# A hybrid decoder layer: another half-product pair, fewer working tiles per attention head, and earlier sums at the output

## The chip, the cores and the metric

The kernel runs on one core of one Trainium2 chip. The metric is the device time of one execution in microseconds (us); smaller is better. The times of before are 1003.48, 1003.79 and 1007.32 us, so the median is 1003.79 us. The profile is of one further execution that took 1006.68 us, with a span of 1005.0 us.

## The reference

One decoder layer on 528 tokens (16 meta tokens and 512 others) of 2048 values. The normed input goes through one input projection; its columns feed three kinds of heads side by side; each head's output is multiplied by its own SiLU gate; all are joined and go through one output projection, and a last norm follows.

```python
h = rms_norm(x, norm_w)
proj = h @ w_in
(dq, dk, dv, dz, db, da, gq, gk, gv, gz, gl, fq, fk, fv, fz, ff) = split_cols(proj)
o_dn  = gated_head_norm(gated_delta_rule_chunked(...), dz, dn_norm_w)     # 6 heads of 128
o_gla = gated_head_norm(gla_chunked(...), gz, gla_norm_w)                 # 5 heads, keys 64, values 128
log_f = log_sigmoid(ff + b_f)
o_fox = forgetting_attention(fq * FOX_D**-0.5, fk, fv, log_f) * silu(fz)  # 5 heads of 128
return x + concatenate([o_dn, o_gla, o_fox]) @ w_out                      # then rms_norm(., final_norm_w)
```

`forgetting_attention` is softmax(q.k + c_t - c_s) over earlier positions, c the running sum of log f, in blocks of 128 queries.

## The kernel before

**Arithmetic.** Everything is float32, made of exact parts: a weight half-block (`raw`, 128 x 1024) becomes a rounded part on ScalarE (`whi`, L165) and the remainder on VectorE (`wlo`, L166), and each product is three matmuls: `xh whi`, `xl whi`, `xh wlo`. The input transposed lies in 16 tiles `xh`, `xl`, one for each 128 of the 2048 values, 528 columns wide; `HT` = 264 is half of them, `NM` = 16 the meta tokens. `load_half` (L144) issues the load of a half-block on the SP queue and the split; the pool `wp` has two buffers, so a third load waits until the first has been split. An ordinary block of 128 columns of `w_in` (`inproj`, L274) takes two half-blocks.

**Pairs by seven products.** For two column blocks of one attention head, `inproj_pair` (L578) does not multiply each by itself. It treats the upper and lower half of the 2048 values, the two token halves and the two blocks as a 2 x 2 by 2 x 2 matrix product, and does it with seven half-size products (`product`, L586, 24 matmuls of 264 columns) instead of eight. The operands are sums: of weights, in `ti` in DRAM, made long ahead by copies and accumulating transfers on the POOL queue; of inputs, in `t1`, `t2`, `t4` (`x_sums`, L541), and, last, `x_last` (L562). The latter overwrites the upper token half of the first eight `xh`, `xl` with a sum, so it comes after every block that still reads the plain input. Per 128 values it issues a load `xe` on the POOL queue, a scaling on ScalarE, a sum on VectorE, a cast on ScalarE into `xh` and a remainder on VectorE into `xl`. The results of the products land in banks of `psb` (four) named `pp_a`, `pp_b` and so on, and are added up into the head's tiles with two half-width intermediates `ta`, `tb` of the tile `tmp`.

**Stages.** Gates, DeltaNet and GLA come first, with their blocks; then the attention ("fox") heads 0 to 4. `fox_head(0)` projects head 0's four blocks in the ordinary way and, in between, the keys and queries (`fk`, `fq`) of head 1. `SKIP = 1` says that this is so: the list `PAIRS` of seven pairs begins with head 1's values and gate (`fv`, `fz`), then (`fk`, `fq`) and (`fv`, `fz`) of heads 2, 3 and 4. While a pair multiplies, the attention of the head before it runs among its matmuls: scores `pfa`, `pfd`, softmax `fp`, transposes `pfx`, output `pfo`. The scores of GLA's third pair of heads (`pss20` to `pss26`, on VectorE the gate differences and weighted keys `gvt`, `gpr`, `kq`) run among head 1's keys and queries. Two working tiles come from the pool `six` (14 buffers) for a head's probabilities, and one more, `fc`, for its gate row `cb`, masked rows `cm` and gate `z`.

**The output.** The first three column blocks of 512 (`pa`, cc 0 to 2) multiply the heads that are done, in four banks of `psb`; then VectorE adds each bank to `accs`, which was loaded with the residual input (`begin`, L1393, `add`, L1416). The rest of the output projection uses seven products too (`pq`, `pr`, `ps`), with weight sums `tw` in DRAM. The norm ends it (L1555 on).

**What sets the order.** Each engine runs its instructions in one fixed order. A scheduler lays that out from the written order and from priorities; weight splits and what is `paced` by them have high priority. On TensorE the products stand as written (`order`), and `PLACE` (L197) says behind which matmul of which block a small matmul may come. The weight-sum transfers are `chores`: each `load_half` allows `rate` units of them (a copy is 1, an accumulation 1.6), and `AHEAD` sets when which are queued and the rate:

```python
AHEAD = {(0, -1): (1.4, (-1, -2, -3, -4, -5, -6, -7), (0, 1, 2, 3))}
tc.add_manual_dep(x.ins, kqs[-1].name, ..., reason="behind")   # x_last: VectorE's part behind GLA's last score
for tb in range(4):
    add(tb, cc, pa[tb])
```

## Time and profile before

| | before |
|---|---|
| median of three runs | 1003.79 us |
| the profiled execution, its span | 1006.68 us, 1005.0 us |
| granted TensorE clock | 0.994 of full |
| TensorE busy | 984.8 us (98%), 7774 matmuls |
| VectorE busy | 658.0 us (65%) |
| ScalarE busy | 478.9 us (48%) |
| GpSimd busy | 251.0 us (25%) |
| gates, DeltaNet, GLA, head 0's blocks | 0 to 612.5 us |
| head 1's keys and queries | 612.5 to 638.5 us |
| the seven pairs | 638.5 to 813.8 us |
| output projection and norm | 813.8 us to the end |

PE is TensorE, DVE VectorE, ACT ScalarE, POOL GpSimd, SP the queue that issues the weight loads. A row of a group gives busy time, mean ns of one, and the idle time before its instructions with what ended it. A row of a timeline gives start, duration, engine, line, operation, output and inputs, and in brackets the idle time before it. Matmuls overlap each other, so the step from start to start, not the duration, is what one costs.

### The profile page before, as it was taken

How to read it: one execution, taken by the hardware profiler on the slowest of the kernel's cores; microseconds unless marked ns; L12 is line 12 of the kernel's file. 1: busy time of each engine (PE TensorE's matmuls, PEld its weight loads, DVE VectorE, ACT ScalarE, POOL GpSimd, SP SyncE). 2: the span in 40 equal slices, each digit the busy share in tenths (PEclk: the TensorE clock that was granted, in tenths of full speed). 3: DMA queues.
4: the chain of work that ended last, by engine and by line, in shares of the span. 5: the costliest groups of instructions: out<-in, count | busy, mean ns of one | idle time of the engine just before them, and what ended most of it. 6: DMA issues, size and time to landing. Idle time of an engine off the chain costs nothing.

```text
span 1005.0 us, 19758 instructions
## 1 busy us (share of the span) xinstructions
PE 984.8 (98%) x7774; PEld 899.4 (89%) x7774; DVE 658.0 (65%) x1427; ACT 478.9 (48%) x1045; POOL 251.0 (25%) x288
## 2 busy tenths in 40 slices
PE   9999999999999999999999999999999998999996
PEld 7899999898999888899999988898999986878885
DVE  5456786966667895335665848666766674968573
ACT  6753534334455244244444445655555552554254
POOL 0031523322233344212223123121212153000060
PEclk9999999999999999999999999999999999999998
DMA  9754666776546798734848685654454558448434
GB/s 338 264 192 165 210 214 234 172 195 158 126 111 171 152 220 220 265 121 149 229 106 218 156 210 161 197 175 145 149 181 145 189 183 296 149 155 272 138 105 168
DMA packets 67489, 186.05 MB, mean 185 GB/s; under 512 B 13725, under 2 KB 16973, under 8 KB 66692
## 3 DMA queue, kind: packets, MB, share of 16 engines
q1 hardware_dynamic: 41920, 121.86, 35.3%
q0 software_dynamic: 16576, 56.83, 23.7%
q10 hardware_dynamic: 8900, 6.10, 2.2%
q8 instruction: 61, 1.00, 0.4%
q14 instruction: 32, 0.26, 0.1%
HBM read 174.07 MB, written 56.69 MB: 230 GB/s over the span
## 4 chain that ended last, share of the span: by engine, by line
PE 80%; DMA 3%; DVE 3%; ACT 2%; issue 1%; POOL 0%; ACTq 0%; POOLq 0%; DVEq 0%
PE pp L260 38%; PE pp_a L592 8%; PE pa L1403 5%; PE pq L1403 4%; PE pt L1403 4%; PE ps L1403 2%; PE pp_b L592 2%; PE pp_d L592 2%; PE pp_c L592 2%; PE pss L1061 1%; PE pr L1403 1%; DMA xb<-in_xT 1%; PE pfo L1283 1%; PE pfa L1249 1%; DVE wlo L166 1%
## 5 line engine op out<-in xcount | busy, mean ns | idle before, releaser
L260 PE MATMUL pp<-xh,wlo 128*128 128x264 f32 (+2 forms) x1120 | 272.3, 306 | 1.4 <-DVE wlo L166 1.4
L260 PE MATMUL pp<-xh,whi 128*128 128x264 f32 (+2 forms) x1120 | 273.4, 306 | 0.2
L260 PE MATMUL pp<-xl,whi 128*128 128x264 f32 (+2 forms) x1120 | 272.8, 306 | 0.0
L165 ACT CAST whi<-raw 128x1024 fp32r<-128x1024 f32 x131 | 137.1, 1047 | 157.7 <-PE pp L260 84.2
L166 DVE TENSOR_TENSOR wlo<-raw,whi 128x1024 fp32r<-128x1024 f32 x131 | 162.0, 1237 | 64.9 <-ACT whi L165 58.3
L260 PEld LDWEIGHTS pp<-xh,wlo 128*128 128x128 f32 x1120 | 182.3, 189 | 10.5 <-DVE wlo L166 1.8
L260 PEld LDWEIGHTS pp<-xh,whi 128*128 128x128 f32 x1120 | 182.3, 188 | 9.8 <-ACT whi L165 0.6
L260 PEld LDWEIGHTS pp<-xl,whi 128*128 128x128 f32 x1120 | 182.5, 189 | 9.0 <-issue 0.4
L405 POOL TENSOR_SCALAR stc<-cv 128x528 f32<-128x528 f32 (+1 forms) x18 | 28.9, 1607 | 146.9 <-DVE cv L633 125.9
L1428 POOL TENSOR_TENSOR accs<-accs,fw 128x512 f32<-128x512 f32 x12 | 17.8, 1521 | 112.1 <-ACT sqf L1425 112.1
L633 DVE SCALAR_TENSOR_TENSOR cv<-pb,cpk,cv 128x528 f32<-128x528 f32 (+1 forms) x54 | 41.1, 761 | 0.8
L592 PE MATMUL pp_a<-t,whi 128*128 128x264 f32 (+1 forms) x224 | 31.9, 291 | 2.0 <-ACT fqk L615 2.0
L592 PEld LDWEIGHTS pp_a<-t,whi 128*128 128x128 f32 x224 | 29.0, 195 | 2.6 <-ACT fqk L615 2.2
L1403 PE MATMUL pa<-whio,oh 128*128 128x512 f32 x72 | 27.0, 408 | 3.7 <-DVE fmt L1261 3.7
L1403 PE MATMUL pa<-whio,ol 128*128 128x512 f32 x72 | 29.3, 407 | 0.0
L1403 PE MATMUL pa<-wloo,oh 128*128 128x512 f32 x72 | 29.1, 404 | 0.0
L165 ACT CAST whis<-raws 128x1024 fp32r<-128x1024 f32 x16 | 16.4, 1049 | 25.0 <-PE pq L1403 8.6
L592 PE MATMUL pp_a<-xh,whi 128*128 128x264 f32 x112 | 28.2, 286 | 0.0
L592 PE MATMUL pp_a<-xl,whi 128*128 128x264 f32 x112 | 28.2, 286 | 0.0
L405 POOL TENSOR_SCALAR stdz<-zdz 128x512 f32<-128x512 f32 x6 | 10.1, 1698 | 62.3 <-DVE zdz L423 62.3
L1210 POOL TENSOR_TENSOR vf<-vf,rstd 128x528 f32<-128x528 f32 x4 | 10.3, 2568 | 58.4 <-DVE vf L619 58.4
L760 DVE TENSOR_TENSOR ab<-ab 51x30 f32<-51x30 f32 (+14 forms) x60 | 21.3, 355 | 4.3 <-DMA ab<-scr 1.8
(487 smaller groups left out, 2129.9 us busy)
## 6 DMA issues: line engine op xcount, KB each, us to landing
raw<-in_w_in SPq DMA_DIRECT2D x103, 512.0 KB, 3.6
ti<-in_w_in POOLq DMA_DIRECT2D x42, 512.0 KB, 5.5
raw<-ti SPq DMA_DIRECT2D x28, 512.0 KB, 3.5
tw<-in_w_dn POOLq DMA_DIRECT2D x24, 512.0 KB, 6.4
ti<-ti POOLq DMA_DIRECT2D x14, 512.0 KB, 6.6
rawo<-in_w_out SPq DMA_DIRECT2D x13, 512.0 KB, 3.6
raws<-tw SPq DMA_DIRECT2D x12, 512.0 KB, 4.6
xt<-in_xtok SPq DMA_DIRECT2D x8, 512.0 KB, 8.9
```

Of the source, the lines that this page charges most:

```text
L165: pace[0] = A.copy(hi, raw).ins
L166: pace[1] = V.tensor_tensor(out=lo, in0=raw, in1=hi.bitcast(F32), op=ALU.subtract).ins
L260: mm = PE.matmul(p_[:, :nt], wt[:, j * m : (j + 1) * m], xx[k][:, t0 : t0 + nt], start=(k == 0 and wt is hi and xx is xh), stop=(k == KT - ...
L405: maxes.append(G.tensor_scalar_max(t, src, LOW).ins)
L592: m = PE.matmul(p_[:, cols], wt[:, j * P : (j + 1) * P], xx[j][part_][:, cols], start=first and i == 0, stop=i == len(todo) - 1, skip_grou ...
L633: V.scalar_tensor_tensor(out=c, in0=pb[:, t0 + w : w + T], scalar=cwc[:, blk, w : w + 1], in1=c, op0=ALU.mult, op1=ALU.add)
L760: V.tensor_tensor(out=t3, in0=a3[:, j + 1 :, j : j + 1].to_broadcast([NN * 4 + H, m, j]), in1=a3[:, j : j + 1, 0:j].to_broadcast([NN * 4 + ...
L1061: mm = PE.matmul(ps[o0 : o0 + n, b * n : b * n + n], kx[rr, k0 : k0 + n], qx[rr, q0 : q0 + n], start=True, stop=True)
L1210: G.tensor_tensor(out=v, in0=v, in1=rstd, op=ALU.mult)
L1249: PE.matmul(pa[:, :m], qT[:, ts], kT[:, :m], start=True, stop=True)
L1403: mm = PE.matmul(p_, o_[:, s], w_, start=(first and n == 0), stop=(last and n == 2), skip_group_check=True)
L1428: G.tensor_tensor(out=acc[tb, cc], in0=acc[tb, cc], in1=fw[cc], op=ALU.mult)
```

## The change

- Head 1's keys and queries become a pair by seven products (`SKIP = 0`, eight pairs, `ti` for eight). In this pair (n = 0) the product `ti[n, 2]` with the replaced input half comes last; `t4`'s product, sixth, has its own bank `e`.
- `x_last` stands right after head 0's gate block and before GLA's third pair of scores on VectorE: now the first gate difference of those scores waits for the last step of `x_last`.
- The scores of GLA's third pair are placed in pair 1, every 16 matmuls; the places of `pfx` are dropped.
- In a pair the copies and sums go to the result tile itself; there is no `tmp`. The third raw buffer is used from pair 2 on, not from pair 1.
- A head has no `fc`: the gate row lies in the middle of the key and query tile, the mask's last block in place, the gate in the tile of the pair's result. The values' transposes move behind the second block of the softmax.
- The transfers of the output's weight sums get a rate of 1.8 from GLA's gates on.
- The sums `acc` of the first output block lie in another pool, are loaded after its second step, and the four adds of cc 0 to 2 have high priority.
- In the last norm the mean and epsilon of the first four parts are taken ahead, and the last 128 columns' squares are summed on VectorE.

```diff
-SKIP = 1
+SKIP = 0
+        "pss21": (('pair', 1), 22),
+        "pss22": (('pair', 1), 38),
...
+        "pg02": (('pair', 1), 118),
-        "pss23": (('fk', 1), 60),
...
-        "pfx43": (('pa', 0), 145),
@@ x_last
-            tc.add_manual_dep(x.ins, kqs[-1].name, ...)
             A.copy(xh[k][:, HT:], x22)
-            V.tensor_tensor(out=xl[k][:, HT:], ...)
+            x = V.tensor_tensor(out=xl[k][:, HT:], ...)
+        tc.add_manual_dep(kqs[0], x.ins.name, ...)
@@ inproj_pair
-    def inproj_pair(n, c1, c2, tmp, each=None):
+    def inproj_pair(n, c1, c2, each=None):
-            hi, lo = load_half(..., raws[0] if third[0] % 3 == 0 and 0 < n and h < FOX_HEADS - 1 else None)
+            hi, lo = load_half(..., raws[0] if third[0] % 3 == 0 and 1 < n and h < FOX_HEADS - 1 else None)
-        A.copy(ta, a[:, :HT])
+        A.copy(c1[:, lo_], a[:, :HT])
...
-        product(a, ti[n, 2], xs_(up, hi_))
-        A.copy(ta, a[:, :HT])
-        V.scalar_tensor_tensor(out=c2[:, hi_], in0=d[:, :HT], scalar=-1.0, in1=ta, ...)
+        def replaced():
+            product(a, ti[n, 2], xs_(up, hi_))
+            A.copy(c2[:, hi_], a[:, :HT])
+            V.scalar_tensor_tensor(out=c2[:, hi_], in0=d[:, :HT], scalar=-1.0, in1=c2[:, hi_], ...)
+        if n > 0:
+            replaced()
         c = bank("c")
         product(c, ti[n, 3], xs_(dn, hi_), True)
+        if n > 0:
+            product(a, w_in[b2, 1], sums("t4"), cols=dead)
+            A.activation(c2[:, dead], a[:, dead], AF.Copy, scale=-1.0)
+        else:
+            e = bank("e")
+            product(e, w_in[b2, 1], sums("t4"), True, cols=dead)
+            A.copy(c2[:, dead], e[:, dead])
+            replaced()
@@ fox_head
+            done["fz", h] = inproj(("fz", h), meta=False)
+            x_last()
             gate_z("fz", h)
-            evac(inproj(("fk", H1)), ahead_[H1][:, 0])
-            evac(inproj(("fq", H1), meta=False), ahead_[H1][:, 2], scale=float(P) ** -0.5)
-            x_last()
-        cc = six.tile([P, 2 * T + S], F32, tag="six", name=f"fc{h}")
+            if b == 1:
+                ...
+                vhi, vlo = values(v)
@@ output
-    AHEAD = {(0, -1): (1.4, (-1, ..., -7), (0, 1, 2, 3))}
+    AHEAD = {(0, -1): (1.4, (-1, ..., -7, -8), (0, 1, 2, 3)), ("gz", 0): (1.8,)}
+        if cc == 0:
+            acc[tb, cc] = part(f"acc{tb}").bitcast(F32)
+            if cc == 0 and kp == 1:
+                for tb in range(4):
+                    begin(tb, cc)
-        for tb in range(4):
-            add(tb, cc, pa[tb])
+        with tc.high_priority(offset=1000000):
+            for tb in range(4):
+                add(tb, cc, pa[tb])
@@ last norm
-            square(tb, 3, c, n)
+            if n < 1:
+                square(tb, 3, c, n)
...
+            V.tensor_tensor_reduce(out=row("sqz")[:, c], in0=a, in1=a, scale=1.0 / D, scalar=r, ...)
+        A.activation(r, r, AF.Ln)
```

More of the change, by code (lines that the diff above doesn't have):

```diff
@@ L1173, in fox_head @@
         qk = tiles[h] = ahead_.pop(h)
-        kT, qT = qk[:, 0], qk[:, 2]
+        kT, cb, qT = (qk[:, i] for i in range(3))
         def values(v):
@@ L1273, in fox_head @@
                 A.copy(p3, px[:, 3 * P :])
+            if b == 1:
+                fs = t15(f"fs{h}")
+                v3, p3, v4 = (fs[:, i] for i in range(3))
+                G.tensor_copy(v4.rearrange("p (b t) -> p b t", t=NM),
+                              v[:, 0:NM].unsqueeze(1).to_broadcast([P, 2 * NB, NM]))
+                vhi, vlo = values(v)
+                if h >= H1:
+                    silu(z, z, f"fz{h}")
+        pm = row(f"ptm{h}", dt=F32R)[:, :S]
+        G.tensor_copy(pm, zero_c.to_broadcast([P, S]))
+        if h < H1:
+            z = row(f"zf{h}")[:, :S]
+            nc.scalar.dma_start(out=z, in_=zd[DN_HEADS + GLA_HEADS + h])
         pw = psm.tile([P, 512], F32, tag="m", name=f"pfw{h}")
-        PE.transpose(pw[:, :P], mt.bitcast(F32).rearrange("p b i t -> p (b i t)"), ident)
+        PE.transpose(pw[:, :P], fm[:, 2].bitcast(F32), ident)
         for b in range(NB):
@@ L1557, in tile_hybrid_trunk @@
             add(tb, 3, p_, c)
-            square(tb, 3, c, n)
-        r = rr[:, tb : tb + 1]
-        V.reduce_sum(r, ss[:, tb, : 3 + cuts], axis=mybir.AxisListType.X)
-        A.activation(r, r, AF.Ln, scale=1.0 / D, bias=eps_c)
+            if n < 1:
+                square(tb, 3, c, n)
+                if tb == 3:
+                    r = rr[:, tb : tb + 1]
+                    V.reduce_sum(r, ss[:, tb, :4], axis=mybir.AxisListType.X)
+                    V.tensor_scalar(r, r, 1.0 / D, EPS, ALU.mult, ALU.add)
+        r = rr[:, tb : tb + 1]
+        if tb < 3:
+            V.reduce_sum(r, ss[:, tb, :4], axis=mybir.AxisListType.X)
+            V.tensor_scalar(r, r, 1.0 / D, EPS, ALU.mult, ALU.add)
+        else:
+            a = acc[tb, 3][:, c]
+            V.tensor_tensor_reduce(out=row("sqz")[:, c], in0=a, in1=a, scale=1.0 / D, scalar=r, op0=ALU.mult,
+                                   op1=ALU.add, accum_out=rr[:, 4:5])
+            r = rr[:, 4:5]
+        A.activation(r, r, AF.Ln)
         A.activation(r, r, AF.Exp, scale=-0.5)
```

119 lines of the change are left out of this document (50 added, 69 removed).

## The prediction

> **What bounds the kernel now.** I read the busy times first, then the tensor engine's waits, then the stretches around the edited places, and last the instructions there.
>
> ```profile
> PE 984.8 (98%) x7774; PEld 899.4 (89%) x7774; DVE 658.0 (65%) x1427; ACT 478.9 (48%) x1045; POOL 251.0 (25%) x288
> PE pa L1403 <- DVE fmt L1261: 3.7, 1, 3.7
> PE pp_a L592 <- ACT fqk L615: 2.0, 1, 2.0
> 612.50:638.50 26.00, 26.00 (x298) 22.83 (x297) 22.86 (x51) 14.86 (x30) 9.45 (x8) 1.00 0.53 157
> 638.50:665.70 27.20, 27.20 (x242) 25.39 (x241) 16.46 (x32) 17.80 (x44) 7.50 (x9) 1.00 0.68 217
> ```
>
> TensorE (PE) is busy 98% of the span, so time goes only where its matmuls get fewer or its waits change. It has two waits worth naming in the second half. The stretches (length, then busy time of PE, its loads, VectorE (DVE), ScalarE (ACT) and GpSimd (POOL), granted clock, DMA share) show where head 1's keys and queries run now: 612.5 to 638.5, PE full, but DVE already at 22.86 of 26 us, 88%. The next stretch holds a pair of seven products; there DVE has room.
>
> **Fewer matmuls.** The two blocks are now 96 matmuls of 264 columns and 48 of 512. Here are the first and last of 18 consecutive 512s, and the first and last of nine consecutive 264s:
>
> ```profile
> 634.05 0.40 PE L260 MATMUL pp<-xh,wlo 128*128 128x512 f32 x1
> 638.00 0.39 PE L260 MATMUL pp<-xl,whi 128*128 128x512 f32 x1
> ...
> 694.13 0.28 PE L592 MATMUL pp_a<-xl,whi 128*128 128x264 f32 x1
> 695.10 0.28 PE L592 MATMUL pp_a<-xl,whi 128*128 128x264 f32 x1
> ```
>
> 3.95 us over 17 steps is 0.232 a step, 0.97 over 8 is 0.121. The old form is 96 x 0.121 + 48 x 0.232 = 22.7 us; the other 154 matmuls of that stretch, the remaining 3.3 us, are small ones of GLA pair 2's scores, which the change moves into the following pair without adding to them. Seven products of 24 matmuls are 168 x 0.121 = 20.3 us: **-2.4 us**.
>
> **What no longer covers pair 0.** Those 20.3 us must now take seven half-block weights instead of four, x_last's eight steps, and GLA's preparation. On ACT, while head 1's keys run, the two half-blocks of its queries are cast among this work before (`whi_0`, `whi_1` those weights, `xe` x_last's rows, `gvt`, `gpr`, `gt` GLA's gates):
>
> ```order
> 539 L165 CAST whi_0_7655<-raw_0_7653 128x1024
> 540 L568 ACTIVATE xe_7715<-xe_7715,cpk 128x264
> 541 L1042 ACTIVATE gvt_6727<-gvt_6727 64x512
> 542 L568 ACTIVATE xe_7721<-xe_7721,cpk 128x264
> ...
> 548 L165 CAST whi_1_7686<-raw_1_7684 128x1024
> ```
>
> The four casts of x_last that follow wait there for DVE, whose part of x_last stands behind the last score; nothing is short. ACT after, up to the second product's weights:
>
> ```order
> 532 L554 CAST xh_131<-xe_7539 128x264
> 533 L551 ACTIVATE xe_7551<-xe_7551,cpk 128x264
> 534 L1002 ACTIVATE gt_6738<-gt_6738 64x528
> 535 L554 CAST xh_138<-xe_7545 128x264
> 536 L1003 ACTIVATE gt_6738<-gt_6738 64x528
> 537 L554 CAST xh_151<-xe_7551 128x264
> 538 L165 CAST whi_3240_7768<-raw_3240_7766 128x1024
> ```
>
> `whi_3240` is product b's weight, `xh` x_last's rounded rows. Three whole steps of x_last moved ahead of it: the weight cast now queues behind a scaling that waits for a POOL-queue load, then behind a cast that waits for DVE, and the weights of products four to six have such steps ahead of them too. DVE's prices:
>
> ```profile
> L166 DVE TENSOR_TENSOR wlo<-raw,whi 128x1024 fp32r<-128x1024 f32 x18 | 22.3, 1241 | 8.3 <-ACT whi L165 8.1
> L569 DVE SCALAR_TENSOR_TENSOR xe<-xe,cpk 128x264 f32<-128x264 f32 x8 | 3.6, 484 | 2.5 <-ACT xe L568 2.5
> L574 DVE TENSOR_TENSOR xl<-xe,xh 128x264 fp32r<-128x264 f32 x8 | 3.1, 424 | 0.1
> L1039 DVE TENSOR_TENSOR gvt<-gqk 64x256 f32<-64x256 f32 x4 | 2.6, 656 | 0.0
> L1009 DVE SCALAR_TENSOR_TENSOR gvt<-gvt,gt 64x528 f32<-64x528 f32 x1 | 0.7, 701 | 1.4 <-ACT gt L1008 1.4
> L1080 DVE TENSOR_TENSOR gt<-gqk 64x512 f32<-64x512 f32 x1 | 0.7, 674 | 0.0
> L1090 DVE TENSOR_TENSOR gdm<-gqk 64x16 f32<-64x16 f32 x1 | 0.2, 156 | 0.0
> L1043 DVE TENSOR_TENSOR kq<-gqk,gvt 64x256 f32<-64x256 f32 x3 | 1.2, 410 | 0.6 <-ACT gvt L1042 0.6
> L1010 DVE TENSOR_TENSOR_SCAN gqk<-gsc,gvt 64x528 f32<-64x528 bf16 x1 | 1.2, 1240 | 0.0
> L423 DVE TENSOR_TENSOR zfz<-pp,rstd 128x512 f32<-128x512 f32 x1 | 0.7, 676 | 0.0
> L608 DVE TENSOR_TENSOR fqk<-pp_b,fqk 128x264 f32<-128x264 f32 x1 | 0.4, 427 | 0.0
> L165 ACT CAST whi<-raw 128x1024 fp32r<-128x1024 f32 x18 | 18.8, 1044 | 13.9 <-issue 4.2 <-PE pp_a L592 4.1 <-DMA raw<-ti 3.4
> ```
>
> Up to the seventh product's weights DVE's order holds six splits (7.4 us), x_last (8 x 0.908 = 7.3), three sums of products (1.3), the fz gate's two operations (1.4) and GLA's scan, ten of its 0.41 us operations and five others (1.24 + 4.1 + 0.66 + 0.70 + 0.67 + 2 x 0.16 = 7.7): 25.1 us. If that starts when fz's product ends at 612.5, the last weights are there at 637.6, and the product's last eight matmuls, which alone read them, take 1.0: 638.6 against 632.8 for PE alone, **+5.8 us**. Low end: the raw buffers.
>
> ```profile
> raw<-ti SPq DMA_DIRECT2D x28, 512.0 KB, 3.5
> 648.33 1.05 ACT L165 CAST whi<-raw 128x1024 fp32r<-128x1024 f32 x1 [1.72 <-DMA raw<-ti]
> ```
>
> Pair 0 has two, and a load, cast, split and some 0.5 of handing over are 3.5 + 1.04 + 1.24 + 0.5 = 6.3 us per two products against 2 x 2.9 = 5.8; that is 1.5 over three such rounds, or nothing if loads run faster than the median (no reason for a gain below). ACT waited for such a load in before's pair 0 already, hidden by score matmuls that pair 0 no longer has. High end: DVE at its 88%, 25.1 / 0.88 = 28.5, so +9.2. I take 5.8: it is the engine's own row. Pair 1 gives up its third raw buffer, but gets GLA's scores, 3.3 us at least: two of its products then last 5.8 + 3.3 x 2/7 = 6.7, above 6.3, so nothing.
>
> **The wait inside the next pair.** Before, the seventh product (248 columns) starts here:
>
> ```profile
> 688.30 3.22 PE L592 MATMUL pp_a<-t,whi 128*128 128x248 f32 x16 [1.97 <-ACT fqk L615]
> 691.32 1.57 PE L592 MATMUL pp_a<-t,wlo 128*128 128x248 f32 x8
> 692.73 0.28 PE L592 MATMUL pp_a<-xh,whi 128*128 128x264 f32 x1
> 690.00:695.00 5.00, 5.00 (x36) 5.00 (x35) 2.72 (x6) 2.31 (x6) 0.00 (x0) 0.76 0.00 0
> ```
>
> PE waits 1.97 us for an ACT copy into half of the shared `tmp`, which waits until a late DVE sum has read that half. Then 24 matmuls take 4.43 instead of 24 x 0.114 = 2.7 us (0.121 x 248/264) at a granted clock down to 0.76: 1.7 more. In place there is no such half; the copy has its own target and a whole product (2.9 us) of time. **-3.7 us**; if the copy is late for other reasons, 0. [...]
>
> **The wait between the first two output column blocks.**
>
> ```profile
> 834.52 0.47 PE L1403 MATMUL pa<-whio,ol 128*128 128x512 f32 x1
> 838.68 0.47 PE L1403 MATMUL pa<-whio,oh 128*128 128x512 f32 x1 [3.68 <-DVE fmt L1261]
> 842.64 0.39 PE L1403 MATMUL pa<-wloo,oh 128*128 128x512 f32 x1
> 834.58 0.31 DVE L1253 CUSTOM_DVE_ANT_0 fp<-pfa,fc 128x144 f32<-128x144 f32 x1 [3.38 <-PE pfa L1249]
> 837.85 0.68 DVE L1418 TENSOR_TENSOR accs<-accs,pa 128x512 f32<-128x512 f32 x1
> ```
>
> 834.52 to 838.68 is 3.9 more than a step; the ten steps to 842.64 take 3.96 instead of 2.3: 5.6 in all. The bank is free only when DVE has added it to `accs`, and that add queues behind head 4's softmax. DVE before, first blocks of head 4, `accs` the output sums:
>
> ```order
> 1087 L166 TENSOR_TENSOR wloo_0_10174<-rawo_0_10171,whio_0_10173 128x1024
> 1088 L1253 ISA fp_9943,fsm_9944<-pfa_9939,fc_9904 128x144
> 1089 L1253 ISA fsm_9944 128x1
> ...
> 1094 L166 TENSOR_TENSOR wloo_1_10218<-rawo_1_10215,whio_1_10217 128x1024
> 1095 L1259 RECIPROCAL fsm_9944<-fsm_9944 128x1
> ...
> 1098 L1418 TENSOR_TENSOR accs_10030<-accs_10030,pa_10036 128x512
> ```
>
> And after, `acc` the same sums:
>
> ```order
> 1100 L166 TENSOR_TENSOR wloa_10603<-rawa_10600,whia_10602 128x1024
> 1101 L166 TENSOR_TENSOR wloo_0_10247<-rawo_0_10244,whio_0_10246 128x1024
> 1102 L1423 TENSOR_TENSOR acc_10172<-acc_10172,pa_10100 128x512
> 1103 L1423 TENSOR_TENSOR acc_10174<-acc_10174,pa_10101 128x512
> 1104 L1423 TENSOR_TENSOR acc_10176<-acc_10176,pa_10102 128x512
> 1105 L1423 TENSOR_TENSOR acc_10178<-acc_10178,pa_10103 128x512
> 1106 L1239 ISA fp_9989,fsm_9990<-pfa_9985,fqk_9355 128x144
> ```
>
> The four adds went from behind the softmax block to ahead of it; the block waits instead, and nothing of PE needs it for a product's length. The first bank is complete some 2 us before the last, so an add of 0.68 is in time: **-5.6 us**, or 0 if the split ahead of it (`wloa`, a new neighbour) waits for its load.
>
> **The rest.** At the end the last square goes from ACT to DVE:
>
> ```profile
> 997.28 0.31 ACT L1425 ACTIVATE sqf<-accs 128x128 f32<-128x128 f32 x1 [0.86 <-DVE accs L1418]
> 997.90 0.29 ACT L1561 ACTIVATE frs<-frs,eps_c 128x1 f32<-128x1 f32 x1 [0.22 <-DVE frs L1560]
> ```
>
> These 0.62 us become one DVE operation, some 0.3 by its size: **-0.3**. At nothing: the eight further weight-sum transfers and the denser ones in GLA (a half-block there lasts 48 x 0.121 = 5.8 us of PE, two buffers give 11.6 for about 5.8 of load, cast and split, so loads may take 5 us longer before PE waits); the missing tile of a head, values() later and the mask in place (POOL at 25%).
>
> **Sum.** -2.4 + 5.8 - 3.7 - 5.6 - 0.3 = -6.2 us against the profiled 1006.7 (span 1005.0, 1.7 outside). The median of the runs, 1003.8, lies 2.9 below the profiled one: **997.6**. With pair 0's ends, 993.3 to 1001.0.
>
> **Rivals.** *A, pair 0 at PE's pace.* DVE's GLA work is done before 612.5 or after, and loads come early: slip 0, total -12.0, 991.8. For it: POOL starts x_last's loads earlier in its order now. Against: DVE's 88%. *C, the output wait stays.* Queues keep the first adds late: -0.6, 1003.2, with slip 9.2 1006.6. For it: a DMA share above 1 there.
>
> ```profile
> 835.00:840.00 5.00, 1.32 (x4) 1.10 (x5) 4.41 (x13) 1.56 (x3) 0.55 (x2) 0.91 1.02 395
> xe<-in_xT POOLq DMA_DIRECT2D x8, 264.0 KB, 4.7
> ```
>
> *D, the clock falls in pair 0.* Several waits near 2 us there, each followed by 1.7 us of slow clock as at 688: three cost 5.1, total -1.1, 1002.7. [...] *B, slower: x_last's loads stand on pair 0's path.* Its rows are shared buffers; a later load starts only when an earlier step has freed one, and takes 4.7 us, with the weight casts queued behind its scaling. Four such reloads are 18.8 us of slip: total +6.8, 1010.6. It is slower than before from a slip of 12.0, two and a half reloads in the open. Against it: ACT and DVE have other work meanwhile. [...]
>
> **Numbers.** About 0.5%, 5 us, is what a measurement of this kernel can tell from none, so the bounds are 998.8 and 1008.8. Forecast 0.42 (0.26 of it below 998.8), A 0.20, C 0.17, D 0.06, B 0.15. Faster 0.46, same 0.39, slower 0.15. The range from A to C's upper end, 991.0 to 1006.6, leaves out B and a little at each edge.
>
> **What would show it.** Pair 0 (the products with ACT's x_last casts among them): PE's waits for `whi` and `wlo` there sum to about 5.8 and DVE is near full. No wait for ACT's copy in the pair after head 1's; no wait above 0.7 us between the first two output blocks, with the clock at 1. Wrong: waits of PE for weights in GLA, or in pair 0 over 12 us.

## The result and the profile after

The changed kernel is slower. Its median is 1019.85 us (1017.39 to 1020.61), beside 1003.89 us for the kernel before on the same chip; the ratio is 1.0146, with a 95% interval of 1.0124 to 1.0168. The profiled execution took 1019.96 us with a span of 1018.2, which is 13.2 above the span of before. The medians stand 16.0 apart because before's profiled execution lay 2.8 above its median and the one of after lies on it. So the prediction (997.6, range to 1006.6) is wrong in direction, and the result lies 13 us above its range. One run reported below, of 1025.43 us in the kernel without `x_last`'s loads, is left out of that kernel's figures as slow: its granted clock was 0.985, that of the nine others 0.989 to 0.994.

First the busy times, then TensorE's waits (total, times, longest), then the two stretches that answer to those shown of before, and a piece of the output part:

```profile
PE 987.3 (97%) x7798; PEld 904.1 (89%) x7798; DVE 672.1 (66%) x1449; ACT 481.0 (47%) x1050; POOL 256.6 (25%) x302
PE pp_d L574 <- ACT whi L165: 3.7, 1, 3.7
PE pfx L1253 <- ACT whia L165: 2.8, 1, 2.8
PE pp_a L574 <- ACT fqk L588: 2.6, 1, 2.6
PE pa L1408 <- DVE acc L1423: 1.8, 1, 1.8
PE psd L1021 <- ACT gvt L965: 1.4, 1, 1.4
619.20:647.80 28.60, 24.00 (x178) 23.52 (x177) 24.24 (x45) 17.38 (x33) 8.80 (x7) 0.88 0.48 160
647.80:676.10 28.30, 28.30 (x376) 26.00 (x375) 17.37 (x37) 15.04 (x34) 3.97 (x3) 1.00 0.56 187
850.00:855.00 5.00, 3.21 (x9) 2.46 (x9) 5.00 (x9) 1.42 (x3) 0.69 (x1) 0.50 0.67 213
```

Both old waits (1.97 for `fqk` in the pair, 3.68 for head 4's softmax at the output) are gone under their old names. Four new ones stand there, 10.9 us together, with one of 1.4 in GLA, and the clock is 0.88 in pair 0 and 0.50 in a piece of the output part. Read from the timelines by the first matmul of each stage, the 13.2 us come from these stages (differences taken before rounding):

| stage (from, to) | before | after | difference |
|---|---|---|---|
| start to head 1's keys | 612.5 | 619.2 | +6.7 |
| head 1's keys and queries (pair 0 after) | 25.9 | 28.6 | +2.7 |
| the next pair (head 1's values and gate) | 27.5 | 28.3 | +0.9 |
| head 2's keys and queries | 26.8 | 27.5 | +0.7 |
| the pairs left | 121.4 | 122.8 | +1.4 |
| first output blocks (`pa` to the first `pq`) | 64.5 | 66.7 | +2.2 |
| output by seven products (`pq` to `pz`) | 116.1 | 115.5 | -0.6 |
| last part and norm | 10.2 | 9.6 | -0.5 |

Half of the loss lies ahead of everything that the prediction priced; the gains that it counted on (-2.4, -3.7 and -5.6) do not show in any row. Ahead of pair 0 there is no single large new wait: TensorE's waits there (above 0.15 us) sum to 11.3 us instead of 6.1, in many small pieces. Three places carry the new large waits. In pair 0 (the first row is the median of `x_last`'s loads, from issue to landing):

```profile
xe<-in_xT POOLq DMA_DIRECT2D x8, 264.0 KB, 3.3
621.51 1.34 POOL L1223 TENSOR_SCALAR_AFFINE_SELECT fqk<-fqk 128x128 f32<-128x128 f32 x1 [1.24 <-DMA fqk<-gd]
622.81 0.73 POOL L549 DMA_DIRECT2D xe<-in_xT  x1
628.85 0.52 ACT L551 ACTIVATE xe<-xe,cpk 128x264 f32<-128x264 f32 x1 [4.36 <-DMA xe<-in_xT]
630.72 1.04 ACT L165 CAST whi<-raw 128x1024 fp32r<-128x1024 f32 x1
631.81 3.89 PE L574 MATMUL pp_d<-t,whi 128*128 128x264 f32 x16 [3.70 <-ACT whi L165]
```

ScalarE stands 4.36 us at a scaling of `x_last` whose rows have not landed; the fourth product's weight cast is queued behind it, and TensorE behind that cast. The load that is late was itself issued late: on GpSimd's queue it stands behind the mask of head 0's attention, which waits 1.24 us for a row of its own. At head 2's keys:

```profile
681.36 0.32 SPq L1151 DMA_DIRECT2D zd<-gqk  x1
685.12 0.38 ACT L588 COPY fqk<-pp_a 128x264 f32<-128x264 f32 x1 [1.69 <-DMA zd<-gqk]
685.56 3.65 PE L574 MATMUL pp_a<-t,whi 128*128 128x264 f32 x16 [2.63 <-ACT fqk L588]
```

The first product's copy now goes straight into the result tile `fqk`, and that tile has the slot of `six` from which GLA's `gqk` is still being stored. GLA's scores were moved one pair later, and so was that store. In the output part:

```profile
825.92 5.52 SPq L1361 DMA_DIRECT2D zr<-zd  x8
846.69 2.41 DVE L1250 TENSOR_SCALAR fp<-fp,fsm 128x128 f32<-128x128 f32 x1
849.25 0.45 PE L1253 MATMUL pfx<-ident,fp 128*128 128x128 f32 x1 [2.77 <-ACT whia L165]
848.22 1.04 ACT L165 CAST whia<-rawa 128x1024 fp32r<-128x1024 f32 x1 [7.17 <-DMA rawa<-in_w_dn]
849.29 1.23 DVE L166 TENSOR_TENSOR wloa<-rawa,whia 128x1024 fp32r<-128x1024 f32 x1
850.44 1.22 DVE L166 TENSOR_TENSOR wloo<-rawo,whio 128x1024 fp32r<-128x1024 f32 x1
851.57 2.48 DVE L1423 TENSOR_TENSOR acc<-acc,pa 128x512 f32<-128x512 f32 x4
852.40 0.76 PE L1408 MATMUL pa<-whio,oh 128*128 128x512 f32 x1 [1.79 <-DVE acc L1423]
```

The four adds were moved ahead of the second softmax block, but they stand behind the split `wloa`, whose weight, queued on SP behind eight loads `zr`, lands 15.7 us after it was issued. The wait of 2.77 us before them belongs to something else than its label: the transpose `pfx` reads `fp`, not `whia`, and the operation on VectorE that makes `fp` ended at 849.10. That operation was late because the one before it lasted 7.77 us (last section).

### The profile page after: what moved, and what is told of

Same layout as the page of the kernel before. It is cut to its first block, busy times and chain, and to the rows that moved or that the text cites. A ratio compares the mean times of both kernels' runs of the same rounds, so it can differ in the third digit from the quotient of the medians.

```text
span 1018.2 us, 19861 instructions
## 1 busy us (share of the span) xinstructions
PE 987.3 (97%) x7798; PEld 904.1 (89%) x7798; DVE 672.1 (66%) x1449; ACT 481.0 (47%) x1050; POOL 256.6 (25%) x302
## 4 chain that ended last, share of the span: by engine, by line
PE 64%; DMA 9%; issue 6%; DVE 5%; ACT 3%; POOL 3%; ACTq 1%; POOLq 0%; DVEq 0%
PE pp L243 23%; PE pp_a L574 8%; PE pq L1408 4%; PE pa L1408 4%; PE pt L1408 4%; PE pp_c L574 2%; PE pp_d L574 2%; PE ps L1408 2%; PE pp_b L574 2%; DMA rawa<-in_w_dn 2%; DMA sc<-ab 1%; DVE wlo L166 1%; PE pr L1408 1%; DMA xb<-in_xT 1%; DMA xe<-in_xT 1%
## 5 line engine op out<-in xcount | busy, mean ns | idle before, releaser
L243 PE MATMUL pp<-xh,wlo 128*128 128x264 f32 (+2 forms) x1072 | 260.0, 305 | 2.6 <-DVE wlo L166 1.9
L243 PE MATMUL pp<-xh,whi 128*128 128x264 f32 (+2 forms) x1072 | 260.8, 306 | 1.7 <-ACT whi L165 1.7
L243 PE MATMUL pp<-xl,whi 128*128 128x264 f32 (+2 forms) x1072 | 260.5, 306 | 0.0
L243 PEld LDWEIGHTS pp<-xh,wlo 128*128 128x128 f32 x1072 | 175.0, 189 | 11.5 <-DVE wlo L166 2.7
L243 PEld LDWEIGHTS pp<-xh,whi 128*128 128x128 f32 x1072 | 174.8, 189 | 10.8 <-ACT whi L165 2.4
L243 PEld LDWEIGHTS pp<-xl,whi 128*128 128x128 f32 x1072 | 175.1, 189 | 8.3 <-issue 0.4
L1433 POOL TENSOR_TENSOR acc<-acc,fw 128x512 f32<-128x512 f32 x4 | 5.7, 1438 | 124.5 <-ACT sqf L1430 124.5
L574 PE MATMUL pp_a<-xh,whi 128*128 128x264 f32 x128 | 32.3, 286 | 0.3 <-ACT vf L592 0.3
L574 PE MATMUL pp_a<-xl,whi 128*128 128x264 f32 x128 | 32.5, 288 | 0.0
L165 ACT CAST whia<-rawa 128x1024 fp32r<-128x1024 f32 x12 | 12.6, 1049 | 26.1 <-DMA rawa<-in_w_dn 7.2
```

The lines of the kernel that those rows point to most:

```text
L165: pace[0] = A.copy(hi, raw).ins
L243: mm = PE.matmul(p_[:, :nt], wt[:, j * m : (j + 1) * m], xx[k][:, t0 : t0 + nt], start=(k == 0 and wt is hi and xx is xh), stop=(k == KT - ...
L574: m = PE.matmul(p_[:, cols], wt[:, j * P : (j + 1) * P], xx[j][part_][:, cols], start=first and i == 0, stop=i == len(todo) - 1, skip_grou ...
L1433: G.tensor_tensor(out=acc[tb, cc], in0=acc[tb, cc], in1=fw[cc], op=ALU.mult)
```

## The experiments

Each ratio is to the kernel before, run on the same chip; start times are read from the profiled execution. What the expectations call head 4's last block is where the stretch `pa` ends, the first product `pq`.

**The weight-sum transfers at their old rate, the rest of the change kept.**

```diff
-    AHEAD = {(0, -1): (1.4, (-1, ..., -8), (0, 1, 2, 3)), ("gz", 0): (1.8,)}
+    AHEAD = {(0, -1): (1.4, (-1, ..., -8), (0, 1, 2, 3))}
```

> The changed kernel, with the weight-sum transfers at their old rate of 1.4 in GLA instead of 1.8; all else stays. In its profile pair 0 starts at 619.2 us, where head 1's keys started at 612.5 before. Theory (traffic): the denser transfers delay other loads, of GLA's input sums and of weights, and PE waits; pair 0 then starts near 614 (eight further transfers stay) and the time falls by some 5 us, to about 1015 us. Rival (order): the 6.7 us come from the changed tiles and order, so pair 0 still starts near 619 and the time stays at 1019 to 1020.

Measured: 1028.39 us (1024.88 to 1031.24), ratio 1.023 [1.0199, 1.026]. Head 1's keys start at 614.8, 4.4 us earlier than in after, but pair 0 and its neighbour then take 60.5 instead of 56.9 us:

```profile
641.29 0.88 POOL L493 DMA_DIRECT2D tw<-tw  x1 [2.10 <-DMA tw<-tw]
635.92 3.77 PE L574 MATMUL pp_e<-t,whi 128*128 128x248 f32 x16 [5.44 <-ACT whi L165]
614.80:644.20 29.40, 23.60 (x169) 22.86 (x167) 20.60 (x38) 15.10 (x29) 13.85 (x15) 0.88 0.98 256
```

The last transfers are issued until 641, in pair 0, with a DMA share of 0.98 there, and the pairs' own weights come late. The theory's start is right and its total wrong. So the denser transfers do cost time ahead of head 1's keys, and with eight pairs they cannot simply be left out: the 4.4 us gained are lost again in these two pairs (3.6) and, beyond that, at head 2's keys, which take 32.8 instead of 27.5 us.

**`x_last` without its loads** (the values of the upper token half are then taken from the rounded rows in SBUF).

```diff
-            nc.gpsimd.dma_start(out=r..., in_=xT[:, k : k + 9 : 8, HT:])
-            A.activation(x12, x12, AF.Copy, scale=nwc[:, k : k + 1])
+            A.activation(x12, xh[k][:, HT:].bitcast(F32), AF.Copy, scale=1.0)
...
```

> The changed kernel, where x_last takes its two rows from the rounded parts that lie in SBUF instead of loading the input again; the same ScalarE and VectorE operations, eight loads fewer on the POOL queue (the sums are then made of rounded parts, so pairs are less exact). Theory (loads): in pair 0 ScalarE waits 4.4 us for such a load with the fourth product's weights queued behind, PE waits 3.7 us and then runs at a low clock; without loads pair 0 falls from 28.6 us to about 23, the time by 5 to 6 us to about 1014. Rival (VectorE): VectorE's 25 us of work hold pair 0 anyway; it stays at 26 us or more, and the gain is under 2.5 us.

Measured: 1012.93 us (nine runs, 1007.13 to 1017.36), ratio 1.0069 [1.0045, 1.0093]; against after's 1.0146 that is 7.7 thousandths, some 8 us, less. The profiled execution, at 1016.15, is only 3.8 us below after's, since its pair 0 began 2.6 us later. Pair 0:

```profile
621.80:644.80 23.00, 21.73 (x178) 21.12 (x177) 21.70 (x42) 15.65 (x28) 6.57 (x4) 1.00 0.40 130
```

23.0 us instead of 28.6, at full clock, with DVE busy 94% of the time, no wait for `whi` there and one of 1.05 us for a `wlo`. The loads and the clock that falls behind their wait are 5.6 us of pair 0; VectorE's work alone lets PE pass at 23.0. The waits at head 2's keys (2.50) and in the output part (2.93, 2.40) stayed, as they should.

**In the kernel before, the fifth product's copy, for which the seventh waits, straight into the result tile.**

```diff
-        A.copy(ta, a[:, :HT])
-        V.scalar_tensor_tensor(out=c2[:, hi_], in0=d[:, :HT], scalar=-1.0, in1=ta, ...)
+        A.copy(c2[:, hi_], a[:, :HT])
+        V.scalar_tensor_tensor(out=c2[:, hi_], in0=d[:, :HT], scalar=-1.0, in1=c2[:, hi_], ...)
```

> The kernel before, with one part of the change: the copy of the fifth product goes into the result's own tile, not into the shared intermediate. Theory (shared half): the 1.97 us wait of the seventh product at 688.3 and the slow clock behind it go, 3.7 us less, about 1000. Rival: the copy waits for something else and moves little; no gain, or a wait of the same size at another product of that pair.

Measured: 1009.0 us (1007.73 to 1012.43), ratio 1.0032 [1.0016, 1.0048]. The wait in the pair fell from 1.97 to 0.47, the pair from 26.8 to 23.7 us (-3.1), and the output part starts 4.6 us earlier; there it loses 8.2:

```profile
832.81 0.33 PE L1190 MATMUL pwf<-ident,v 128*128 128x128 f32 x1 [1.88 <-POOL v L1188]
836.89 0.45 PE L1267 MATMUL pfx<-ident,fp 128*128 128x128 f32 x1 [3.25 <-DVE fmt L1262]
841.20 0.80 PE L1404 MATMUL pa<-whio,oh 128*128 128x512 f32 x1 [2.96 <-DVE accs L1419]
```

The mechanism of the prediction's -3.7 is right. But one edited line made the scheduler lay out the output part anew: before, 17 to 28 output matmuls stand between most of the dependent steps of head 4's first softmax blocks; here (the matmuls in their order on TensorE, with the counts of the output and value matmuls)

```text
before: pa 21, pfo, pvf, pa 3, pfo 12, pa 17, pwf, pfa, pfd, pa 28, pfx, pfa, pfd, pa 27
here:   pa 11, pfo, pvf, pfo 12, pwf, pfa, pfd, pfx, pfa, pfd, pa 26
```

they come in one piece, with nothing to cover the chain.

**In the kernel before, the four adds ahead of the next split, and head 4's second softmax block behind them.**

```diff
+        if (cc, kp) == (1, 1):
+            tc.add_manual_dep(pace[1], last_add[0], ..., reason="behind")
...
+            tc.add_manual_dep(softmax[-3].ins, x.ins.name, ..., reason="behind")
```

> The kernel before, with VectorE's four adds of the first output block put ahead of the next weight split and of head 4's second softmax block. Theory (queue): PE's 3.7 us wait between the first two output blocks is VectorE's order; with the adds ahead it goes with its slow clock, 5.6 us less, about 998. Rival (loads): the adds then wait for the residual's loads, which compete with other transfers at a DMA share above 1, and the wait stays at 2 us or more; or the delayed softmax gives PE another wait.

Measured: 1002.91 us (1000.84 to 1005.65), ratio 0.9982 [0.9965, 1.0]. The wait of 3.68 became 0.67 (`833.51`), and the stretch `pa` to `pq` 59.4 instead of 64.5 us; but twelve attention matmuls now come behind the first `pq`, so that `pq` to `pz` grew from 116.1 to 119.2. Net -2.0: of the 5.1 us gained at the wait 3.0 are given back, since work that had stood in it has to stand elsewhere. The interval of the total reaches 1.0, so that the total alone would not show a gain.

**The change with head 1's keys and queries as ordinary blocks** (seven pairs, `x_last` and the scores where before has them).

```diff
-SKIP = 0
+SKIP = 1
...
```

> The changed kernel, but head 1's keys and queries are two ordinary 512-column blocks again, with x_last after them and GLA pair 2's scores inside them as before; seven pairs instead of eight, and the weight-sum transfers of seven pairs ahead. All else of the change stays (denser transfers in GLA, pairs in place, no seventh tile, the output part). Theory (pair 0's form is a cost of its own: x_last's loads and the weights' queue): from the start of head 1's keys to the next pair 53.4 us as in the kernel before instead of 56.9, total 3 to 5 us below the changed kernel, about 1015. The start of head 1's keys stays near 619, since the denser transfers stay. If the wait of 2.6 us at head 2's keys comes from the slot that the moved scores hold, it goes too, and the total is about 1011. Rival (the rest of the change holds all of the loss, and pair 0 as a pair was a gain hidden by it): 1018 or more.

Measured: 1009.52 us (1002.58 to 1015.2), ratio 1.0028 [0.9997, 1.006]. From the keys to the next pair's end 53.9 us (626.7 to 680.6), as in before (53.4), so the theory holds there; at head 2's keys no wait is left (23.6 us). The rival is out: with pair 0's form and what it moves, four fifths of the loss go (1.0146 to 1.0028). Not expected were a start of head 1's keys at 626.7 in the profiled execution (waits of 4.35 us at 407 and 2.67 at 501, with the dense transfers still there) and an output part without a wait (56.5 us): the edit also changed where the scheduler puts head 4's attention. So not all of the difference is pair 0's.

**The change without the third buffer for raw weights**, which rotates the slots of `six`.

```diff
-            raws.append(six.tile([P, 1024], F32, tag="six", name="raw3"))
-            V.memset(raws[0][:, 0:1], 0.0)
```

> The changed kernel without the third buffer for raw weights in the pairs. It takes a slot of the pool that also holds the pairs' first products and GLA's scores, so the slots rotate differently and head 2's first product no longer gets the slot whose old tile is stored by a late transfer. Theory (the 2.63 us wait at head 2's third product is that slot): the wait and the slow clock behind it go, head 2's keys 26 instead of 30 us, and of that -4 us the missing raw buffer gives nothing back, since two products there last as long as a load, a cast and a split: about 1015. Rival 1 (another late tile's slot, or the two raw buffers alone, 6.3 us per two products of 5.8, cost it again): the total stays within 2 us of the changed kernel's, 1017 to 1021, with waits of 0.5 to 1.5 us for weights in many pairs.

Measured: 1017.41 us (1015.81 to 1021.89), ratio 1.0111 [1.0062, 1.0161]. TensorE's wait of 2.63 is gone and head 2's keys take 23.2 us instead of 27.5, as the theory has it (the copy still waits, for GLA's own operation and no longer for its store, and is in time); the output part then waits longer:

```profile
682.29 0.38 ACT L588 COPY fqk<-pp_a 128x264 f32<-128x264 f32 x1 [2.09 <-DVE gqk L1148]
683.68 2.12 PE L574 MATMUL pp_a<-t,whi 128*128 128x264 f32 x16
845.54 1.04 ACT L165 CAST whia<-rawa 128x1024 fp32r<-128x1024 f32 x1 [7.78 <-DMA rawa<-in_w_dn]
849.72 0.77 PE L1406 MATMUL pa<-whio,oh 128*128 128x512 f32 x1 [5.95 <-DVE acc L1421]
```

The output started 3.3 us earlier, the weight `rawa` landed only 2.7 earlier, and TensorE met the adds behind it: a single wait of 5.95 us. That the slot was the cause at head 2's keys is shown. The total cannot choose between the theory's 4 us and rival 1's 2 or less: the ratio fell by 3.5 thousandths, with an interval of 10; rival 1's mechanism, waits for weights in many pairs, did not come.

**The change with its output part in another order**: the adds ahead of `wloa`, the cast `whia` behind the second block's first cast, the loads `zr` one step later.

```diff
-    steps = [...] + [load_zr]
+    steps = [...] + [lambda: None, load_zr]
+        if nw[0] == 3:
+            tc.add_manual_dep(pace[1], last_add[0], ..., reason="behind")
+            tc.add_manual_dep(pace[0], cast[0], ..., reason="behind")
```

> The changed kernel with three places of the output part moved: the four adds of the first column block stand ahead of the split wloa, the first cast of a lower weight (whia) behind the second block's first cast, and the loads of the gate sums one step later, away from GpSimd's sums. Theory (the output part's 2.8 and 1.8 us waits come from the weight load behind which the adds and casts queue): both go with the slow clock behind them, the stretch from the first output block to head 4's last block shrinks from 66.7 to about 60, total about 1013. Rival 1 (the loads and GpSimd's sums beside VectorE set the place, whatever stands first in the queues): the waits stay above 3 us in sum and the total within 2 us of 1019. Rival 2: the waits go but come back behind the last heads' products; the stretch up to the last products shrinks by under 2 us, total 1017 or more.

Measured: 1017.23 us (1013.24 to 1022.42), ratio 1.012 [1.0062, 1.0178]; the profiled execution took 1013.24. In its trace the lower weight is as late as ever, and TensorE does not wait:

```profile
845.57 1.05 ACT L165 CAST whia<-rawa 128x1024 fp32r<-128x1024 f32 x1 [6.81 <-DMA rawa<-in_w_dn]
840.77 2.77 DVE L1423 TENSOR_TENSOR acc<-acc,pa 128x512 f32<-128x512 f32 x4 [0.76 <-PE pa L1408]
```

`pa` to `pq` is 59.2 instead of 66.7, `pq` to `pz` 119.9 instead of 115.5, net -3.1. So here a lower weight that keeps ScalarE waiting 6.81 us costs TensorE nothing, since the adds do not stand behind its split. The totals of four runs spread over 9 us, so that they alone do not tell -2.6 from nothing.

**The same without the later `zr` loads** (only the last three lines of that diff).

> The changed kernel with two of the three moves in the output part that were tried together: the four adds ahead of the split wloa, and the lower weight's first cast (whia) behind the second block's first cast; the loads of the gate sums stay where the change has them, so that GpSimd's sums again run in one piece while VectorE works on head 4's softmax. Theory 1 (the load of the lower weight, behind which the adds stood, was the whole cause): the stretch from the first output block to head 4's last block is about 59 us as with all three moves, with no wait of TensorE above 1 us in it. Theory 2 (VectorE's small softmax operation beside GpSimd's sums is a cause of its own): if GpSimd's sums run back to back there, an operation of VectorE that takes 0.23 us elsewhere lasts until GpSimd's last one ends, 5 us or more, the adds stand behind it, TensorE waits 2 to 4 us, and the stretch is 62 to 66 us.

Measured: 1019.61 us (1014.12 to 1021.3), ratio 1.0116 [1.0075, 1.0157]; `pa` to `pq` 61.3.

```profile
831.47 0.65 SPq L147 DMA_DIRECT2D rawo<-in_w_out  x1
845.84 1.05 ACT L165 CAST whio<-rawo 128x1024 fp32r<-128x1024 f32 x1 [4.86 <-DMA rawo<-in_w_out]
848.99 0.47 PE L1408 MATMUL pa<-whio,oh 128*128 128x512 f32 x1 [1.99 <-DVE acc L1423]
```

Neither theory had this: now the second block's own weight, issued behind the eight `zr` loads at 831.5 (at 825.9 with the later `zr`), lands late, and the adds stand behind its split. So the adds' place and the order of the loads go together: with the adds moved, TensorE still waits 1.99 us, since another split ahead of them waits. VectorE's softmax operations ended 0.4 us ahead of GpSimd's sums this time and were not held, so theory 2 was not put to the test.

**The kernel before with the third, the fourth and the tail's edit together.**

> The kernel before with three edits that the two singles and the change suggest: the seventh product's copy straight into the result tile, the four adds of the first output block ahead of the next split together with head 4's second softmax block behind them, and the last square on VectorE as in the change. Theory (the two waits are independent gains, the first one's give-back in the output part came from the late adds, which are moved here): -3.1 in the pair, -2 to -5 in the output part, -0.6 at the end, about 997 to 999. Rival (with the pairs ahead by 3 us the output part starts before its loads have landed, as when the copy alone was moved, whatever the order of the adds): the first gain is given back there, total 1003 to 1005.

Measured: 1009.68 us (1005.35 to 1013.37), ratio 1.003 [1.0006, 1.0054]. The rival is right that the gain is given back, the time lies above its 1003 to 1005 (by the ratio too), and the reason is the bunched order of the single edit again:

```profile
832.18 0.33 PE L1192 MATMUL pwf<-ident,v 128*128 128x128 f32 x1 [1.70 <-POOL v L1190]
836.26 0.45 PE L1270 MATMUL pfx<-ident,fp 128*128 128x128 f32 x1 [3.30 <-DVE fmt L1265]
```

The output part starts 5.0 us earlier; `pa` to `pq` is 4.4 and `pq` to `pz` 2.9 longer. The wait for the adds themselves is down to 0.79.

**The kernel before with only the denser transfers.**

```diff
-    AHEAD = {(0, -1): (1.4, (-1, ..., -7), (0, 1, 2, 3))}
+    AHEAD = {(0, -1): (1.4, (-1, ..., -7), (0, 1, 2, 3)), ("gz", 0): (1.8,)}
```

> The kernel before with one number added: the weight-sum transfers get denser from GLA's gates on (1.8 instead of 1.0), as in the change; seven pairs' transfers, all else as before. Theory (the denser transfers by themselves delay GLA's own weight loads, and that is most of the 6.7 us by which the changed kernel reaches head 1's keys later): head 1's keys start at 616 to 620 instead of 612.5, the pairs run as before, total 4 to 7 us above the kernel before. Rival 1 (the transfers alone cost nothing; the delay needs the eighth product's further transfers, or x_last's and the scores' new places): start within 1 us of 612.5, total within 2 us. Rival 2 (transfers that are done ahead of the pairs shorten the pairs by as much as GLA grows): start later, but the output part no later than 814 + 2 us.

Measured: 1014.85 us (1012.79 to 1020.07), ratio 1.0086 [1.0059, 1.0114]. Head 1's keys start at 618.3 instead of 612.5, the output part at 820.4 instead of 814.1, `pz` at 1000.9 instead of 994.8: one delay of 6 us in DeltaNet and GLA, and from there on the same lengths. The first two lines are before's and this kernel's 400 to 500 us, the others this kernel's:

```profile
400.00:500.00 100.00, 100.00 (x891) 93.61 (x890) 46.17 (x110) 40.80 (x123) 20.70 (x31) 1.00 0.62 190
400.00:500.00 100.00, 97.01 (x848) 89.90 (x847) 44.25 (x107) 40.02 (x121) 23.63 (x32) 0.98 0.69 183
487.56 0.49 DVE L557 SCALAR_TENSOR_TENSOR xb<-xb,cpk,xa 128x264 f32<-128x264 f32 x1 [2.23 <-DMA xb<-in_xT]
490.12 0.27 ACT L946 ACTIVATE sqo<-po 128x128 bf16<-128x128 f32 x1
493.83 0.33 PE L871 MATMUL pt<-ident,on 128*128 128x128 f32 x1 [2.99 <-ACT on L957]
```

The norm of DeltaNet's output (`sqo`), which the transposes `pt` need, now stands on ScalarE behind steps of the input sums, whose rows POOL's queue loads: it starts at 490.1, where before it ran ahead of the last of them at 486.9. TensorE waits 2.99 us for its result. (The rate before is 1.4, as in the diff, not the 1.0 of the expectation.) That the density alone costs this time is shown, and rivals 1 and 2 are out; that it is GLA's own weight loads that are delayed, as the theory says, is not: the one large wait is for DeltaNet's norm. The profiled executions of all kernels here agree on the density: head 1's keys start at 616.1 to 626.7 in the eight with the dense transfers, at 610.4 to 613.6 in before and the four built on it without them, and at 614.8 in the change at the old rate. What stays open is how much of the 6 us is the traffic (DMA share 0.69 for 0.62, a `tw` load 7.4 instead of 6.4 us) and how much the order: the rate also moves instructions of all engines in that part, and no run has the one without the other.

**The change with three places mended** (no `x_last` loads, no third raw buffer, the other output order; the rounded values as above).

> The changed kernel with three of the edits tried alone together: x_last's rows from SBUF instead of its eight loads (the values of the last columns are then rounded ones), no third buffer for raw weights, and the output part's adds, cast and gate-sum loads moved. The denser transfers stay. Theory (the loss is the sum of four separate places, and three of them are mended): pair 0 23 us instead of 28.6, head 2's keys 23 instead of 27.5, output part 59 instead of 66.7, together -17 of 1018, about 1001, that is some 4 us below the kernel before, with the delay of GLA left in it. Rival (a place mended is given back at the next one: what comes earlier finds its loads not landed): above 1007, with new waits for weights in the pairs or the output part.

Measured: 1007.96 us (1004.13 to 1013.52), ratio 1.0012 [0.9989, 1.0034]; the profiled execution took 1004.53, near the fast end of its runs, with a span of 1002.8.

```profile
616.10:639.10 23.00, 21.68 (x178) 21.07 (x177) 21.73 (x42) 15.66 (x28) 6.58 (x4) 1.00 0.42 129
674.89 2.12 PE L573 MATMUL pp_a<-t,whi 128*128 128x264 f32 x16
```

By its trace, against before: +3.6 ahead of head 1's keys, pair 0 -2.9, the next +1.7, head 2's keys -3.7, the pairs left +2.2, `pa` to `pq` -6.0, `pq` to `pz` +3.6, the end -0.5: -2.2 us. All three places behave as the theory says, and no group of waits above 2.1 us in sum is left. The ratio falls from 1.0146 to 1.0012, so the three places hold most of the loss. But the theory's 4 us below the kernel before lie outside the interval, which contains 1, and the median lies in the rival's range (above 1007): part of what is gained is given back, in this trace in the pair behind pair 0, in the pairs left and behind the first `pq`.

**The kernel before with the adds' and the tail's edit alone.**

> The kernel before with the two edits that kept their gain: the four adds of the first output block ahead of the next split with head 4's second softmax block behind them, and the last square on VectorE as in the change. Theory: -2 from the adds as in the single, -0.5 at the end, ratio to the kernel before 0.997 to 0.998. Rival (the gain of the adds was within the runs' scatter): 1.000 or above.

Measured: 1003.77 us (1000.99 to 1008.14), ratio 0.9969 [0.9952, 0.9985]: as the theory has it, and faster than both kernels. It keeps two of the ideas of the change and none of its pair 0.

## Why the prediction was wrong, point by point

**The step that failed first: "At nothing: the eight further weight-sum transfers and the denser ones in GLA".** It was allowed 5 us of spare time for TensorE's weight loads, and that account left out the other loads on POOL's queue, the engines' queues behind them, and the new order. Alone, in the kernel before, the density costs 6 us; in the changed kernel the same stretch is 6.7 longer. The sign of error that the prediction gave, waits of PE for weights in GLA, is there only weakly: in after three waits for `whi` ahead of pair 0 sum to 1.7 us, and the longest wait of GLA, the `psd` of 1.4, is not for a weight.

**Pair 0: the term of +5.8 was to make its 20.3 us of matmuls 26.1; it took 28.6, and for another reason.** VectorE was not the limit (busy 85% in pair 0): with nearly the same work and the loads gone, the pair takes 23.0 us, so of the +5.8 at most 2.7 is VectorE's. The 5.6 above that are one reload of `x_last` (4.36 us of ScalarE, 3.70 of TensorE) and the clock after it, 0.88 for the pair. That is rival B's mechanism at the price of one reload, with rival D's. Pair 0 and the next pair together were forecast 3.4 us longer (-2.4 + 5.8) and are 3.5 longer, 56.9 for 53.4: that agreement is luck. The rival's chance was put too low because "ACT and DVE have other work meanwhile" was said of queues that run in order, where it did not help: in after ScalarE stood 4.36 us ahead of the scaling, with the weight cast behind it. Rival B's price for a load, 4.7 us, is the median of before. The median of the eight loads in after was 3.3 us, but the one that counted was issued at 622.8 and let the scaling start at 628.9, 6 us. The 0.5 us of handing over in the term's low end is the author's estimate, and no run shows it: in before's pair a split begins 0.03 us behind its cast's end (649.38, 649.41), and the next load is issued 0.02 behind the split's end (650.64, 650.66).

**-3.7 at head 2's keys: mechanism right, place taken.** In the kernel before the copy's own target gave -3.1, in the change with three places mended -3.7. In the change the very move that frees the copy of `ta` binds another copy to a slot that is free too late; the prediction had named the case ("if the copy is late for other reasons, 0") and not looked whose slot the tile would get.

**-5.6 at the output: the condition set there came true.** "Or 0 if the split ahead of it (`wloa`, a new neighbour) waits for its load": it waited, 7.17 us on ScalarE. The wait of 2.77 us just ahead, for a softmax operation held on VectorE, was in no term; in the trace it fills time in which the adds could not have started anyway. And the size was too large even where the adds come in time: -2.0 in the kernel before, -3.1 in the change, because matmuls that had filled the old wait come later instead.

**-0.3 at the end** held: -0.5. **-2.4 for fewer matmuls** held as a count (7 x 24 = 168 of the 178 matmuls in pair 0).

**Rivals.** A needed loads that come early and is out. C had the outcome of the output part; its 1003.2 still counted the gains elsewhere. B alone had the direction, for pair 0's reason; its 1010.6 left out the loss ahead of pair 0. The direction was lost because every gain was taken in its favourable branch, though the text itself names the other branch of two of them, and because the one term without a price was the largest loss.

## What to carry to other kernels

Work moved into spare DMA time was not free where an engine's in-order queue held a step that waits for a load (in pair 0 it cost ScalarE 4.36 us and TensorE 3.70, in the kernel before with the denser transfers TensorE 2.99): ask which instruction stands right behind each such step, on ScalarE and VectorE as well as on the queue that issues the load. When a copy or a tile is given another home, look up whose slot it gets and when that is freed. And where a scheduler lays out the program, price an edit on its new order as a whole: here one edited copy ahead of the output gained 3 us at its place and lost 8 in the order that followed from it.

## What the runs showed of the hardware that was not expected

**A wait had no fixed price in clock.** The prediction put 1.7 us of slow clock behind each wait of about 2 us. At head 2's keys the same wait came in several kernels. The first two rows are the change and the kernel with the other output order, each with the 16 matmuls that follow the wait; the last two show the granted clock (third number from the end) around them:

```profile
685.56 3.65 PE L574 MATMUL pp_a<-t,whi 128*128 128x264 f32 x16 [2.63 <-ACT fqk L588]
683.67 2.21 PE L574 MATMUL pp_a<-t,whi 128*128 128x264 f32 x16 [2.75 <-ACT fqk L588]
685.00:690.00 5.00, 4.44 (x24) 4.45 (x25) 1.00 (x5) 1.09 (x2) 0.77 (x2) 0.66 0.47 159
683.00:688.00 5.00, 4.33 (x36) 4.33 (x37) 2.11 (x11) 1.97 (x4) 0.77 (x2) 1.00 0.49 159
```

One paid 1.4 us more, at a granted clock of 0.66, the other nothing, at 1.00; nor did two further kernels, after 2.50 and 2.75 us. The wait that was paid for, of 2.63 us, lies between those that were not, and in before a clock of 0.76 followed on one of 1.97 us. So the length of the wait alone does not tell whether the clock falls; what decides it no run shows.

**VectorE's small operation lasted as long as GpSimd's run of sums.** An operation of 0.23 us (the median of its 20 in the change) took 7.77, ending 0.04 after GpSimd's last sum (847.61 + 1.40 = 849.01):

```profile
841.28 7.77 DVE L1247 TENSOR_SCALAR fm<-fp,fsm 128x16 fp32r<-128x16 f32 x1
841.74 2.81 POOL L649 TENSOR_TENSOR zr<-zr 128x256 f32<-128x256 f32 x4
847.61 1.40 POOL L650 TENSOR_TENSOR zr<-zr 128x256 f32<-128x256 f32 x2
```

Without `x_last`'s loads it was the next operation, of 0.28 us elsewhere, that took 7.85, to 0.08 after GpSimd's last; without the third raw buffer the same one took 2.67, to 0.04 after the end of a shorter run. In the change the small operation lasted for the whole unbroken run of GpSimd's ten operations (841.74 to 849.01) and not for one of 0.7 us. At two other places there it took 1.34 us (702.75) and 1.10 (730.56), to 0.03 and 0.04 after the end of one GpSimd operation of 1.33 and 1.51, though GpSimd went straight on with another. These coincidences speak for a hold of GpSimd on these operations; its cause and what ends it no run took apart. TensorE's wait for `pfx` comes with the two long holds (2.77 and 2.93 us) and is absent in three other kernels built on the change, where the same place has a hold of 2.67 us or none. But in the change's output part the late weight alone suffices for the two waits together: where the hold was 2.67 us, the adds alone cost 5.95.
